# Neighbourhood attention by row groups: taking the groups in twos per head pair, with shared bias tables and keys

## The chip, the core and the metric

One core of one Trainium2 chip runs the whole kernel in one launch, on float32 inputs. The metric is the device time in microseconds (us) of one execution; the time given is the median of the runs. Engines: PE (matrix multiply; PEld is its weight load), DVE (vector), ACT (scalar), POOL (GpSimd), SP (issues nearly all DMAs).

## The reference

One layer (DEPTH is 1): RMSNorm, one projection to q, k, v and gate, 2-D neighbourhood attention on a grid of 32 rows by 64 columns (16 heads of 64), SiLU gate, output projection, residual, final RMSNorm. Shapes: x is (1, 2048, 1024), the projection is 1024 by 4096. Each query sees 8 key rows and 16 key columns around it, with a learned bias per head and offset.

```
def row_fn(r):
    rs = jnp.clip(r - kh // 2, 0, rows - kh)          # kh = 8 key rows
    qr = ...[query row r];  kr, vr = ...[key rows rs .. rs+7, columns around the block]
    s = jnp.einsum('bnqhd,bknjhd->bhnqkj', qr, kr).astype(jnp.float32) * scale
    row_off = rs + jnp.arange(kh) - r + NA_ROWS - 1
    bias = jnp.take(col_bias, row_off, axis=1).transpose(0, 2, 3, 1, 4)
    s = jnp.where(col_valid[None, None], s + bias[None], NEG_INF)
    p = jax.nn.softmax(s.reshape(B, H, nb, NA_QBLOCK, kh * NA_KBLOCK), axis=-1)
    o = jnp.einsum('bhnqkj,bknjhd->bnqhd', p, vr)
x = x + (o * jax.nn.silu(gate)) @ w_out               # then the final rmsnorm
```

## The kernel before

Two stages of projections come first (`stage_one`, `stage_two`, 0 to 562 us of the profiled execution): dense 512-column matmuls in a seven-product scheme, whose results q, k, v and gate go to DRAM (`qd`, `kd`, `vd`, `sgd`). At the end the output projection runs in the same scheme (`rows_by_seven`, from about 878 us). Between them lies the attention stage, 32 **runs**; between the attention's own matmuls a fixed number of dense matmuls is put, first the rest of the projections (`projections`: q, k and gate of head pairs 6 and 7 for the lower half of the grid, 288 matmuls), then the first four output tiles (`outputs`, 192 matmuls).

A run is one head pair `p` (0 to 7) and one **row group** `T` (0 to 3: the 8 query rows 8T to 8T+7 with all 64 columns, 512 queries). A run has two halves of 4 query rows, two quads of 8-column strips, two heads `s`. Its steps:

- `load_k`, `load_q`, `load_v`, `load_sg`, `load_bias` bring keys, queries, values, gate and bias tables by SP. Keys of a run are the key rows `KEY_ROWS[T]`: 11, 15, 15 or 12 rows, each row 64 columns, so (rows x 64 + 8) x 4 bytes x 128 partitions. `kp` has two buffers for them. Bias tables are of three kinds (`TABLES`: "mid" with 11 key rows by 23 columns, "top" and "end" with 8 by 23), one table per quad; group 0 needs top and mid, groups 1 and 2 mid alone, group 3 mid and end. Group 2 takes the tables that group 1 of the same head pair has loaded; the others load all of theirs.
- `scores(i)` for each quad: 16 small matmuls per call and head pair into two banks, then per half and head one `tensor_tensor_reduce` on DVE (line 1314): bank plus bias table goes to the tile `X`, with the row minimum into `st`. The bank is read in its own order (key row outer, column inner, contiguous) and `X` is written column outer, key row inner, so with a step of 11, 12 or 15 elements. Then ACT takes the exponential (line 1320) in place.
- `normalise` multiplies by the reciprocal of the sums (POOL, DVE and ACT, lines 1332 to 1336), `turns` transposes `X` on PE (line 1354, into banks `ph`) and copies to `pta` (DVE and ACT, lines 1358 and 1360), `values` multiplies by `vt` (line 1377), DVE multiplies by the gate into `og` (line 1381), and `keep` stores `og` to `ogd` (SP, line 1384).
- `clear_x` sets to zero (POOL) the parts of `X` that a group's halves don't write. It is called at the start, and where the group's kind changes (two times).

The loop over `m` emits, in this order: `begin(m)` (puts the loads of the next run on a list by due time, counted in dense matmuls), dense matmuls, the rest of `normalise` of run m-1, dense matmuls, `turns(m-1)`, `scores(2m)`, `scores(2m+1)` with `normalise(2m)` in it, `values(m-1)`. So an engine's order is the order written out, and SP issues its DMAs strictly in the order in which their due times came: per run the store of `ogd` (it waits for DVE's `og`), `vt`, tables `em`, `q`, `kt`, `sgt`, and between them what else is due.

The order of runs is

```
order = [(p, 0) for p in range(NP)] + [(p, T) for p in range(NP) for T in (1, 2)] + [(p, 3) for p in range(NP)]
```

and the number of dense matmuls per run is `amount[m]`, 13.5, with 1.5 more or less in turn in runs 8 to 23 (`amount[m] += 1.5 if m % 2 == 0 else -1.5`). The first output tiles need row group 0 of all head pairs: `load_og(0)` and `load_og(1)` (512 KB each, line 1411) are called in the last half of `projections`, `split_og(0)` is put on the list 24 matmuls later with a lag of 9. In the last runs `land_first` and `land_rest` load parts of the output weights into buffers that the attention no longer uses.

Of the kernel before, what the change touches and what calls it, by code (L numbers as in the profile page):

```python
# [22 lines left out]
NK = D // 128  # L23
# [11 lines left out]
KEY_ROWS = [(0, 11), (4, 19), (12, 27), (20, 32)]  # L35
HALF_ROWS = [[(0, 8), (0, 11)], [(0, 11), (4, 11)], [(0, 11), (4, 11)], [(0, 11), (4, 8)]]
# [7 lines left out]
def bias_tables(rpb):  # L44
    out = []
    for q0, k0, n in TABLES.values():
        for quad in range(2):
            got = []
            for g in range(4 * quad, 4 * quad + 4):
                qr, col, kr, c = np.ogrid[q0:q0 + 4, :8, k0:k0 + n, :WIDE]  # L50
# [11 lines left out]
def build(ctx, tc, x, xr, xt, wg, bias, w_out, n0, nf, out):  # L62
# [21 lines left out]
    kp = pool("kp", 2)  # L84
# [4 lines left out]
    def vh(shape, dt, nm):  # L89
        if not vhalf:  # L90
            t = vp([128, 1024], dt, nm)
            vhalf.extend((t[:, :512], t[:, 512:]))
        return vhalf.pop(0)

# [508 lines left out]
    def stage_one():  # L603
# [6 lines left out]
        land["x12"] = [rbp([128, 512], F32, "land") for _ in range(2)] + [kp([128, 1024], F32, "land")[:, :512] for _ in range(2)]  # L610
# [30 lines left out]
        def value_rows(j):  # L641
            spot = mkp([128, 3, 512], F32, "vs")
            homes = [spot[:, k] for k in range(3)] + [kp([128, 1024], F32, "vs")[:, :512]]
# [49 lines left out]
        def step(i):  # L693
# [3 lines left out]
            if i >= 2 * E:  # L697
                seven.after(n, P, then)
            elif P == 1:
                seven.keep(n, kp([128, 1024], F32, "p1")[:, :512] if n > 3 else accs[n - 2] if n > 1 else None)  # L700
# [205 lines left out]
        def load_u1():  # L906
            for t in range(4):
                U1[t] = accs[t] if t < 2 else ep([128, 512], F32, "u1") if t == 2 else kp([128, 1024], F32, "u1")[:, :512]
                nc.sync.dma_start(U1[t], vu1[t])
# [87 lines left out]
    def stage_two():  # L997
# [11 lines left out]
        def out_rows(k):  # L1009
            def g():  # L1010
# [3 lines left out]
                else:  # L1014
                    homes = [rbp([128, 512], F32, "ow") for _ in range(2)]
                homes += [kp([128, 1024], F32, "ow")[:, :512] for _ in range(4 - len(homes))]
# [31 lines left out]
        def also(n, i):  # L1048
            if (n, i) in sums_at:
                sums_at[n, i]()  # L1050
            if n == 0:
                if i == 0:
                    load_ahead()
                elif i == 1:
                    for f in load_bias(0, 0):
                        f()
# [4 lines left out]
                if i == 3:  # L1061
                    load_k(0, 0)()
                    load_q(0, 0)()
# [14 lines left out]
        def values_product(P, i):  # L1078
            if P in (1, 6, 5):
# [5 lines left out]
            if P == 1:  # L1085
                U1[i] = ep([128, 512], F32, "u1") if i < 2 else kp([128, 1024], F32, "u1")[:, :512]
# [117 lines left out]
    order = [(p, 0) for p in range(NP)] + [(p, T) for p in range(NP) for T in (1, 2)] + [(p, 3) for p in range(NP)]  # L1204
    pairs = [(p, T, quad) for p, T in order for quad in range(2)]
    lastp = {T: p for p, T in order}

    def slot(T, p):
        return 7 if p == lastp[T] else p - (p > lastp[T])

    def load_k(p, T):
        r0, r1 = KEY_ROWS[T]
        n = (r1 - r0) * GW
        must(*[("k", p, c) for c in range(r0 // 8, (r1 + 7) // 8)])

        def keys():
            KT[p, T] = t = kp([128, 1024], F32, "kt")
            more = 8 * (r1 < ROWS)
            if not more:
                nc.gpsimd.memset(t[:, n:n + 8], 0.0)  # L1220
            nc.sync.dma_start(t[:, :n + more], kd[p][:, r0 * GW:r1 * GW + more])
# [12 lines left out]
    def load_v(p, T):  # L1234
        r0, r1 = KEY_ROWS[T]
# [3 lines left out]
        nc.sync.dma_start(t[:8 * (r1 - r0)], rows)  # L1239
# [6 lines left out]
    kinds_of = lambda T: {0: ("top", "mid"), 3: ("mid", "end")}.get(T, ("mid", "mid"))  # L1246

    def load_bias(p, T):
        fs = []
        for kind in dict.fromkeys(kinds_of(T)):  # L1250
            w = 2 * WIDE * TABLES[kind][2]
            for quad in range(2):
                t = mp([128, 512], F32, "em")[:, :w]
                for half in range(2):
                    if kinds_of(T)[half] == kind:
                        EM[p, T, quad, half] = [t[:, :w // 2], t[:, w // 2:]]
                o = TABLE_AT[kind] + quad * w
                fs.append(lambda t=t, o=o, w=w: nc.sync.dma_start(t, bias[p, :, o:o + w]))
        if T == 1:
            for quad in range(2):  # L1260
                for half in range(2):
                    EM[p, 2, quad, half] = EM[p, 1, quad, half]
# [4 lines left out]
    def height(T):  # L1267
        return KEY_ROWS[T][1] - KEY_ROWS[T][0]

    def by_column(t, half, T):  # L1270
        u, n = HALF_ROWS[T][half]
        return t[:, :WIDE * height(T)].rearrange("p (c r) -> p c r", r=height(T))[:, :, u:u + n]

    def make_x():
        for half in range(2):
            for quad in range(2):
                for s in range(2):
                    X[quad, half, s] = xp([128, 512], F32, f"x{s}")
        clear_x(0)

    def clear_x(T):
        R = height(T)
        for quad in range(2):
            for half, (u, n) in enumerate(HALF_ROWS[T]):
                a, b = (0, u) if u else (n, R)
                for s in range(2):
                    t = X[quad, half, s]
                    nc.gpsimd.memset(t[:, WIDE * R:(WIDE + 1) * R], 0.0)
                    if a < b:
                        nc.gpsimd.memset(t[:, :WIDE * R].rearrange("p (c r) -> p c r", r=R)[:, :, a:b], 0.0)  # L1290

    def scores(i, between=None):
        p, T, quad = pairs[i]
        kt, qt = KT[p, T], QT[p, T]
        both = [bank(512, f"s{s}") for s in range(2)]
        places = {}
        for half, (u, n) in enumerate(HALF_ROWS[T]):
            for s in range(2):
                places[half, s] = both[s][:, 256 * half:256 * half + WIDE * n]
            for h in range(4):  # L1300
                g = 4 * quad + h
                for s in range(2):
                    a = slice(s * 64, s * 64 + 64)
                    o = u * GW + 8 * FIRST[g]
# [4 lines left out]
        for half, (u, n) in enumerate(HALF_ROWS[T]):  # L1309
            xs_ = [by_column(X[quad, half, s], half, T) for s in range(2)]  # L1310
# [587 lines left out]
```

## Time and profile before

| | |
|---|---|
| time before, median of 3 runs | 997.99 us (995.85 to 999.03) |
| the profiled execution: time, span | 1001.41 us, 999.5 us |
| PE busy | 980.3 us (98%) |
| DVE busy | 782.0 us (78%) |
| ACT busy | 531.7 us (53%) |
| POOL busy | 126.7 us (13%) |
| moved by DMA | 233.94 MB, mean 234 GB/s |
| attention stage | about 562 to 878 us |

Matmuls are pipelined and their ends are modelled, so a PE that is called busy can still lose a little beside a wait. A window's row gives its length, then each engine's busy time with its instructions in brackets, the granted TensorE clock, the mean busy share of the 16 DMA engines and what they moved. A row of a group gives what it writes and reads, partitions by elements, the count, the busy time and the mean time of one in ns, and the engine's idle time before them.

### The profile page before, as it was taken

To read this page: it belongs to the slowest core of one execution; us is meant where nothing else is said; L and a number is where in the kernel's file an instruction comes from. 1 tells how busy PE (TensorE), PEld (TensorE's weight loads), DVE (VectorE), ACT (ScalarE), POOL (GpSimd) and SP (SyncE) were. 2 spreads that over 40 slices of the span, in tenths; PEclk is the share of its full clock that TensorE was granted. 3 is DMA by queue.
4 is the path that set the end of the run, shared out by engine and by line. 5 is a ranking of instruction groups with operands and counts; after the bars stand their busy time and mean duration, and the time that the engine had idled before them with its cause. 6 is when DMAs were issued, how large, how long until landed. Compare 5 with 4: busy or idle time off the path is not lost.

```text
span 999.5 us, 22147 instructions
## 1 busy us (share of the span) xinstructions
PE 980.3 (98%) x8172; PEld 797.8 (80%) x8172; DVE 782.0 (78%) x1703; ACT 531.7 (53%) x1310; POOL 126.7 (13%) x256
## 2 busy tenths in 40 slices
PE   9999999999999999999999999999899999999997
PEld 6888888888888888888888777877677777888886
DVE  5899888987666876766775688888789989986866
ACT  7863245455534433333434476777677776653443
POOL 0000001321100000000000122322122321202110
PEclk9999999999999999999999999999999999999999
DMA  8943547777957845655565899988979999997754
GB/s 291 337 132 91 194 146 248 242 249 262 360 144 225 261 136 181 220 180 189 193 206 176 258 327 302 293 237 258 299 223 287 265 285 287 350 364 202 201 148 116
DMA packets 151084, 233.94 MB, mean 234 GB/s; under 512 B 13568, under 2 KB 66048, under 8 KB 150976
## 3 DMA queue, kind: packets, MB, share of 16 engines
q1 hardware_dynamic: 147952, 227.41, 71.7%
q0 software_dynamic: 2592, 4.72, 2.8%
q8 instruction: 64, 1.05, 0.4%
q10 hardware_dynamic: 432, 0.40, 0.1%
q14 instruction: 44, 0.36, 0.1%
HBM read 166.42 MB, written 66.06 MB: 233 GB/s over the span
## 4 chain that ended last, share of the span: by engine, by line
PE 87%; DMA 9%; ACT 2%; SPq 1%; issue 1%; DVE 0%; POOL 0%; ACTq 0%; POOLq 0%; DVEq 0%
PE pp L432 40%; PE pv L598 13%; PE py L1675 11%; PE o L1377 5%; PE s L1305 4%; DMA kt<-kd 3%; PE ph L1354 3%; PE pv L713 2%; PE pp L378 2%; PE pp L376 2%; PE pp L380 2%; ACT x L1320 1%; DMA t<-wodT 1%; DMA xr<-in_x_dram 1%; DMA sgt<-sgd 1%
## 5 line engine op out<-in xcount | busy, mean ns | idle before, releaser
L432 PE MATMUL pp<-h,f 128*128 128x512 f32 x576 | 185.3, 389 | 0.0
L432 PE MATMUL pp<-t,f 128*128 128x512 f32 x702 | 171.4, 389 | 0.0
L432 PEld LDWEIGHTS pp<-t,f 128*128 128x128 f32 x702 | 131.8, 188 | 27.4
L1320 ACT ACTIVATE x<-x,st 128x253 f32<-128x253 f32 (+1 forms) x256 | 124.4, 491 | 45.7 <-DVE st L1314 45.6
L1314 DVE CUSTOM_DVE_ANT_0 x<-s,em 128x253 f32<-128x253 f32 (+1 forms) x256 | 119.0, 576 | 11.8 <-issue 9.9
L432 PEld LDWEIGHTS pp<-h,f 128*128 128x128 f32 x576 | 108.1, 188 | 22.5
L432 PE MATMUL pp<-l,f 128*128 128x512 f32 x288 | 112.1, 389 | 0.0
L1336 POOL TENSOR_SCALAR x<-x,st 128x253 f32<-128x253 f32 (+1 forms) x160 | 75.8, 492 | 224.4 <-DVE st L1325 209.0
L415 DVE TENSOR_TENSOR f<-raw,f 128x512 fp32r<-128x512 f32 x105 | 75.7, 726 | 19.3 <-ACT f L414 19.2
L1377 PEld LDWEIGHTS o<-pta,vt 120*64 120x64 f32 (+2 forms) x1152 | 70.2, 137 | 20.4 <-issue 12.2
L1377 PE MATMUL o<-pta,vt 120*64 120x192 f32 (+8 forms) x1152 | 84.3, 299 | 1.7 <-issue 1.0
L414 ACT ACTIVATE f<-raw 128x512 fp32r<-128x512 f32 x105 | 63.6, 622 | 37.0 <-DVE raw L421 22.0
L1305 PE MATMUL s<-kt,q 64*32 64x253 f32 (+1 forms) x2048 | 61.3, 369 | 9.3 <-DMA kt<-kd 5.7
L1358 DVE COPY pta<-ph 120x512 f32<-120x512 f32 (+2 forms) x96 | 60.2, 681 | 10.8 <-PE ph L1354 10.4
L1360 ACT ACTIVATE pta<-ph 120x512 f32<-120x512 f32 (+2 forms) x96 | 50.2, 594 | 31.1 <-PE ph L1354 31.0
L432 PEld LDWEIGHTS pp<-l,f 128*128 128x128 f32 x288 | 54.0, 188 | 11.4
L1675 PE MATMUL py<-woh,f 128*128 128x512 f32 x192 | 60.9, 390 | 0.0
L598 PE MATMUL pv<-wh,t 128*128 128x512 f32 x176 | 56.2, 389 | 0.0
L1354 PEld LDWEIGHTS ph<-ident,x 64*120 64x120 f32 (+2 forms) x1536 | 46.2, 128 | 11.7 <-issue 8.5
L1305 PEld LDWEIGHTS s<-kt,q 64*32 64x32 f32 x2048 | 39.2, 107 | 19.7 <-issue 4.7
L432 PE MATMUL pp<-sixths,f 128*128 128x512 f32 x198 | 52.7, 389 | 0.0
L1354 PE MATMUL ph<-ident,x 64*120 64x64 f32 (+2 forms) x1536 | 50.9, 219 | 0.3 <-POOL x L1336 0.3
(230 smaller groups left out, 1871.3 us busy)
## 6 DMA issues: line engine op xcount, KB each, us to landing
raw<-in_wg_dram SPq DMA_DIRECT2D x124, 256.0 KB
em<-in_bias_dram SPq DMA_DIRECT2D x48, 253.0 KB
row<-in_xr_dram SPq DMA_DIRECT2D x32, 256.0 KB
vd<-v SPq DMA_DIRECT2D x32, 256.0 KB
sgd<-sg SPq DMA_DIRECT2D x32, 256.0 KB
q<-qd SPq DMA_DIRECT2D x32, 256.0 KB
sgt<-sgd SPq DMA_DIRECT2D x32, 256.0 KB
ogd<-og SPq DMA_DIRECT2D x32, 256.0 KB
```

The costliest lines, as they stand in the source:

```text
L414: nc.scalar.activation(t[:, 0], src, AF.Copy)
L415: nc.vector.tensor_tensor(t[:, 1], src, t[:, 0].bitcast(F32), OP.subtract)
L432: nc.tensor.matmul(B[n, P], t[:, int(m == 2), c], x[k][int(m == 1)], start=P in (1, 6, 5) and k == 0 and m == 0, stop=k == 3 and m == 2, s ...
L598: nc.tensor.matmul(p, a[:, o], b, start=P in (1, 6, 5) and k == 0 and m == 0, stop=k == 3 and m == 2, skip_group_check=True)
L1305: nc.tensor.matmul(places[half, s][h * 32:h * 32 + 32], qt[a, g * 64 + half * 32:g * 64 + half * 32 + 32], kt[a, o:o + n * GW].rearrange(" ...
L1314: nc.vector.tensor_tensor_reduce(xs_[s].rearrange("p c r -> p r c"), flat(places[half, s]), flat(EM[p, T, quad, half][s]), -1.0, 1e38, OP. ...
L1320: nc.scalar.activation(xs_[s], xs_[s], AF.Exp, bias=st[:, o:o + 1], scale=-1.0, accum_out=st[:, 4 + o:5 + o])
L1336: nc.gpsimd.tensor_scalar(t, t, st[:, o:o + 1], 1.0, op0=OP.mult, op1=OP.mult)
L1354: nc.tensor.transpose(ph[h][:k, o:o + 64], X[quad, half, s][q, at:at + k], ident[q, q])
L1358: nc.vector.tensor_copy(o, i_)
L1377: nc.tensor.matmul(o[s * 64:s * 64 + 64, g0 * 64:g1 * 64], vt[:k, strip, s * 64:s * 64 + 64], moving, start=strip == 0, stop=strip == 7, s ...
L1675: nc.tensor.matmul(B[m, P], t[:, a, c], b, start=P in (1, 6, 5) and k == 0 and i == 0, stop=k == 3 and i == 2, skip_group_check=True)
```

## The change

- The order of runs: per head pair first group 1, then group 0, for all eight; then group 2 and group 3 in the same way, with the last two head pairs as (6,2), (7,2), (7,3), (6,3).
- Bias tables: each run loads one kind only (`BRINGS`), two tables: group 1 and 2 mid, group 0 top, group 3 end; groups 0 and 3 take mid from the run before.
- Keys: groups 1 and 0 of a head pair share one key tile, rows 0 to 18; group 1 loads rows 4 to 18, group 0 adds rows 0 to 3. Groups 2 and 3 share rows 12 to 31 (16 rows, then 4). The tile lies in `kp` (now one buffer of 2048 columns) for even head pairs and in `mkp` for odd ones. Elsewhere the two halves of that one buffer (`kh`) stand in for the two buffers of before.
- One frame: every run takes 15 key rows for `X`, the transposes and the values (`FRAME`, `TALL`), in place of 11, 15, 15 and 12. The halves' key rows stay 8 or 11.
- `tensor_tensor_reduce` writes `X` in its own order (key row inner, runs of 8 or 11 elements side by side) and reads the bank with a step of 23 elements; the tables are stored column outer, key row inner, so they are read in order.
- `clear_x` is called in each run, for the rows alone that the last group wrote and the next doesn't.
- `ogd` is in the order of head pairs (`slot` goes). `amount` is even, and the last entry 6 less. `load_og(0)`, `load_og(1)` get a lag of 20, `split_og(0)` one of 19 in place of 9. `land_first` loads 9 parts in place of 10, `land_rest` 8 in place of 7.

```diff
-KEY_ROWS = [(0, 11), (4, 19), (12, 27), (20, 32)]
-HALF_ROWS = [[(0, 8), (0, 11)], [(0, 11), (4, 11)], [(0, 11), (4, 11)], [(0, 11), (4, 8)]]
+FRAME, TALL = [0, 4, 12, 17], 15
+HALF_ROWS = [[(0, 8), (0, 11)], [(0, 11), (4, 11)], [(0, 11), (4, 11)], [(3, 11), (7, 8)]]
...
-    kp = pool("kp", 2)
+    kp = pool("kp", 1)
...
+    def kh(shape, dt, nm):
+        if not khalf:
+            t = kp([128, 2048], dt, nm)
+            khalf.extend((t[:, :512], t[:, 1024:1536]))
+        return khalf.pop(0)
...
-                        load_og(0)
-                        load_og(1)
+                        store(("ogl",), 20, lambda: (load_og(0), load_og(1)))
                     else:
-                        store(("og0",), 9, lambda: split_og(0))
+                        store(("og0",), 19, lambda: split_og(0))
...
-    order = [(p, 0) for p in range(NP)] + [(p, T) for p in range(NP) for T in (1, 2)] + [(p, 3) for p in range(NP)]
+    order = [(p, T) for p in range(NP) for T in (1, 0)] + [(p, T) for p in range(NP - 2) for T in (2, 3)]
+    order += [(NP - 2, 2), (NP - 1, 2), (NP - 1, 3), (NP - 2, 3)]
...
+    PARTS = {1: (4, 19, 8), 0: (0, 4, 0), 2: (12, 28, 0), 3: (28, 32, 0)}
...
         def keys():
-            KT[p, T] = t = kp([128, 1024], F32, "kt")
-            more = 8 * (r1 < ROWS)
-            if not more:
-                nc.gpsimd.memset(t[:, n:n + 8], 0.0)
-            nc.sync.dma_start(t[:, :n + more], kd[p][:, r0 * GW:r1 * GW + more])
+            if T in (1, 2):
+                khalf.clear()
+                KT[p, T // 2] = (kp([128, 2048], F32, "kt") if p % 2 == 0 else mkp([128, 1536], F32, "kt"))[:, :1344]
+            t = KT[p, T // 2]
+            if T == 2:
+                nc.gpsimd.memset(t[:, 1280:1288], 0.0)
+            nc.sync.dma_start(t[:, a - base * GW:b - base * GW], kd[p][:, a:b])
...
+    BRINGS = {0: "top", 1: "mid", 2: "mid", 3: "end"}
...
     def clear_x(T):
-        R = height(T)
+        stale = []
+        for half in range(2):
+            (u0, n0), (u1, n1) = held[half], HALF_ROWS[T][half]
+            held[half] = u1, n1
+            stale += [(half, a, b - a) for a, b in ((u0, min(u0 + n0, u1)), (max(u0, u1 + n1), u0 + n0)) if a < b]
         for quad in range(2):
-            ...
+            for half, a, n in stale:
                 for s in range(2):
-                    ...
+                    nc.gpsimd.memset(by_column(X[quad, half, s], (a, n)), 0.0)
...
-                nc.vector.tensor_tensor_reduce(xs_[s].rearrange("p c r -> p r c"), flat(places[half, s]), flat(EM[p, T, quad, half][s]), -1.0, 1e38,
+                nc.vector.tensor_tensor_reduce(xs_[s], places[half, s].rearrange("p (r c) -> p c r", c=WIDE),
+                                               table[s].rearrange("p (c r) -> p c r", c=WIDE), -1.0, 1e38,
                                                OP.add, OP.min, st[:, o:o + 1])
...
-        k = 8 * (KEY_ROWS[T][1] - KEY_ROWS[T][0])
+        k = 8 * TALL
...
-        if m + 1 < cycles and order[m + 1][0] == 0 and order[m + 1][1] in (1, 3):
+        if m + 1 < cycles:
             clear_x(order[m + 1][1])
...
-    for m in range(8, 24):
-        amount[m] += 1.5 if m % 2 == 0 else -1.5
...
-            if (*nx, 0, 0) not in EM:
-                later_loads(load_bias(*nx), 3, 1.5)
+            later_loads(load_bias(*nx), 3, 1.5)
```

More of the change, by code (lines that the diff above doesn't have):

```diff
@@ L1054, in also @@
                 elif i == 1:
[L1055 removed]
+                    for f in load_bias(*order[0]):
                         f()
@@ L1572, in outputs @@
             p = bank(512, "po")
-            who = {slot(n // 4, q): q for q in range(NP)}
             for i in range(NK):
                 gh, gl = G[n][i]
-                q = who[i]
-                while (q, j) not in woh:
+                while (i, j) not in woh:
                     consume(1, True)
@@ L1633, in load_rows_of @@
         T, i = divmod(n, 4)
-        must(*[("og", p, T) for p in range(NP) if slot(T, p) // 4 == half])
+        must(*[("og", p, T) for p in range(NP) if p // 4 == half])
         A[m, f] = (home or raw)([128, 512], F32, "raw")
```

105 lines of the change are left out of this document (48 added, 57 removed).

## The prediction

> **What bounds the kernel now.** I read the page's first part, then the busy times by stretch, then the chain of waits, then the groups of the attention stage.
>
> ```profile
> span 999.5 us, 22147 instructions
> ## 1 busy us (share of the span) xinstructions
> PE 980.3 (98%) x8172; PEld 797.8 (80%) x8172; DVE 782.0 (78%) x1703; ACT 531.7 (53%) x1310; POOL 126.7 (13%) x256
> ```
>
> PE works nearly all the time, and the change takes no matmul away. So only PE's idle time can be won, 19.2 us in all. The stretches show where it lies: before attention, the four blocks of eight attention runs, and the end.
>
> ```profile
> 0.00:562.00 562.00, 560.57 (x2467) 461.55 (x2475) 422.58 (x679) 255.31 (x484) 32.00 (x37) 1.00 0.66 213
> 561.90:641.40 79.50, 77.57 (x1290) 61.38 (x1289) 64.79 (x206) 56.64 (x178) 18.86 (x44) 1.00 0.95 303
> 641.40:719.90 78.50, 74.80 (x1296) 58.87 (x1293) 66.57 (x204) 57.75 (x176) 20.82 (x55) 1.00 0.92 268
> 719.90:800.10 80.20, 76.53 (x1292) 59.77 (x1293) 69.84 (x210) 58.52 (x179) 20.77 (x58) 0.98 0.88 259
> 800.10:864.70 64.60, 63.33 (x1137) 51.27 (x1138) 58.38 (x202) 44.28 (x150) 16.05 (x41) 1.00 0.95 297
> 864.70:999.50 134.80, 127.56 (x710) 105.09 (x708) 99.80 (x204) 59.31 (x146) 18.16 (x23) 0.99 0.73 218
> ```
>
> Length minus PE's busy time gives 1.4 us ahead of attention, then 1.93, 3.70, 3.67 and 1.27 (10.6 us in the attention blocks), and 7.2 at the end, mostly the tail behind the last matmul. In attention the DMA engines are busy 88 to 95% of the time; elsewhere 66 to 73%. What PE waits for:
>
> ```profile
> PE s L1305 <- DMA kt<-kd: 5.7, 5, 2.8
> PE s L1305 <- issue: 3.5, 2, 2.7
> PE o L1377 <- issue: 1.0, 1, 1.0
> PE o L1377 <- ACT pta L1360: 0.8, 1, 0.8
> PE ph L1354 <- POOL x L1336: 0.3, 1, 0.3
> ```
>
> So the loss is keys that land late. Single attention runs, from one group of scores to the next, show how it is spread (the first two are group 0; then groups 1, 2, 2, 2, 1, 2):
>
> ```profile
> 584.68:594.78 10.10, 8.92 (x165) 7.14 (x162) 8.88 (x28) 7.71 (x24) 2.26 (x5) 1.00 1.03 342
> 594.78:605.18 10.40, 9.65 (x162) 7.45 (x162) 6.58 (x24) 5.72 (x20) 2.25 (x5) 1.00 0.89 278
> 659.96:668.88 8.92, 8.92 (x165) 7.04 (x161) 7.38 (x25) 7.25 (x23) 2.44 (x5) 1.00 0.77 218
> 668.88:678.48 9.60, 9.60 (x168) 7.60 (x164) 8.67 (x27) 7.22 (x23) 2.44 (x5) 1.00 0.91 254
> 687.39:698.62 11.23, 10.22 (x167) 7.79 (x164) 9.20 (x28) 7.87 (x24) 2.45 (x5) 1.00 0.89 251
> 708.22:719.92 11.70, 8.99 (x164) 7.06 (x161) 9.16 (x27) 7.48 (x23) 2.46 (x5) 1.00 1.02 324
> 719.92:730.48 10.56, 10.56 (x160) 7.97 (x160) 7.04 (x24) 6.08 (x20) 2.45 (x5) 0.84 0.84 232
> 787.67:800.13 12.46, 9.69 (x167) 7.38 (x163) 11.38 (x31) 8.34 (x25) 3.66 (x23) 1.00 0.97 263
> ```
>
> A clean run has no PE idle at all: 8.92 us for group 1, 9.60 for group 2 with three matmuls more, so 0.23 us per dense matmul. A disturbed one loses 0.8 to 2.8 us of idle and a little more, since a matmul drawn across a stall counts as busy (10.22 us at 687 with one matmul less than the clean 9.60: 0.6 hidden). After the long stall at 717 the granted clock was 0.84 and that run took 10.56 in place of 8.92: 1.6 us more.
>
> **The change, part by part.**
>
> **Bytes.** Sizes follow from the code (columns x 512 bytes), and three rows anchor them:
>
> ```profile
> em<-in_bias_dram SPq DMA_DIRECT2D x48, 253.0 KB
> ...
> kt<-kd SPq DMA_DIRECT2D x16, 484.0 KB
> vt<-vd SPq DMA_DIRECT2D x16, 480.0 KB
> ```
>
> Tables before, per head pair: three pairs of mid (6 x 253), one of top and one of end (4 x 184), 2254 KB; after, two pairs of mid and one each of top and end, 1748. Keys: 356 + 484 + 484 + 384 = 1708 KB; after, 484 + 128 + 512 + 128 = 1252. Values: 352 + 480 + 480 + 384 = 1696; after, 4 x 480 = 1920. Net 738 KB less per head pair, 5.9 MB of some 85 MB that the four attention blocks move (their GB/s times their lengths): 7%. Fewer DMAs too: 64 tables in place of 80.
>
> Per run, with queries, gate and the store of the output (768 KB): before 2350, 2238, 1732, 2410 KB for groups 0 to 3; after 1744, 2238, 2266, 1744. So the heavy blocks, where each run asks for 2.4 MB, go, and everything looks like the middle blocks of today, where 2.24 and 1.73 alternate. That lightens the first and the last block, and the change of block at 787 to 800, where keys waited behind four tables. It doesn't lighten the middle. I take as gone the idle of the two group-0 runs (1.18 + 0.75), of the run at 787 (2.77) and of the last block (1.27), 6.0 us, and 1.2 hidden beside it (0.3 for each of four stalls, half of the 0.6 above): -7.2. Bounds: nothing, if each is replaced by a stall of the middle kind, and all 10.6 + 1.6 + hidden 2 = -14.2.
>
> **What stays.** The worst stall of the middle, with SP's issues ahead of it (start, length):
>
> ```profile
> 708.19 0.90 SPq L1411 DMA_DIRECT2D ograw<-ogd  x2
> 709.13 0.65 SPq L1221 DMA_DIRECT2D kt<-kd  x1
> ```
>
> Keys queue behind 1 MB for the output tiles, and scores come 2.7 us late (the 708 row), with the slow clock behind it: 4.3 us. The new lag of 20 moves these two loads to a run or two later, since group 0 now ends with run 15. There they stand right behind the store of run 15's `ogd`, which they must see landed; SP stands still for that time, and queued behind it are that run's `q` and `kt`. So I keep 4.3 us (bounds 1 and 7), and the 1.0 at 687 and smaller ones. What is late next is the keys of groups 1 and 2, still the last large DMA of each burst. Against the change: their burst now falls into a run of 13.5 dense matmuls with a group 0 or 3, about 9 us, before into one of 9.60.
>
> **Splits.** `split_og(0)` is now emitted 5 matmuls ahead of its use (before 15), which is 1.1 us, and its copies stand in ACT's and DVE's queue ahead of a `normalise`. Before, one split cost PE 0.3 us (last row of the waits above). I take +0.7, bounds 0 and 2.
>
> **Transposes** get 15 rows everywhere:
>
> ```profile
> L1354 PE MATMUL ph<-ident,x 64*120 64x64 f32 x768 | 26.2, 221 | 0.3 <-POOL x L1336 0.3
> ...
> L1354 PE MATMUL ph<-ident,x 64*96 64x64 f32 x384 | 12.4, 218 | 0.0
> L1354 PE MATMUL ph<-ident,x 64*88 64x64 f32 x384 | 12.3, 218 | 0.0
> ```
>
> 384 transposes of 120 columns hold PE 13.1 us, of 96 12.4, of 88 12.3. Nothing hides PE's own work: +1.5 us. Scores keep their halves of 8 and 11 rows. Values contract over 120 rows in place of 88 or 96 with the same moving columns: nothing.
>
> **Strided bank reads.** Today's read of the bank is in order and the write to `X` steps 44 to 60 bytes; after, the read steps 92 bytes and the write is in order.
>
> ```profile
> L1314 DVE CUSTOM_DVE_ANT_0 x<-s,em 128x253 f32<-128x253 f32 x192 | 97.1, 606 | 9.6 <-issue 8.3 <-PE s L1305 1.0
> ...
> L445 DVE TENSOR_TENSOR u<-pp,p 128x512 f32<-128x512 f32 x38 | 26.1, 687 | 13.2 <-PE pp L432 13.1
> ...
> L421 DVE TENSOR_TENSOR s<-raw 128x512 f32<-128x512 f32 x21 | 14.4, 685 | 4.9 <-DMA raw<-in_wg_dram 4.9
> ```
>
> Line 445 reads a bank with a step of 8 elements (32 bytes) and takes 687 ns for 512, as line 421 does from contiguous SBUF: a strided bank read is free there. Line 1314 takes 606 ns for 253, far more per element, so its strided write may be what costs. Per run it holds DVE 3.91 us, and ACT's exponentials behind it 4.12:
>
> ```profile
> 668.88:678.48 9.60, 3.91 (x16) 1.00 0.91 254
> 668.88:678.48 9.60, 4.12 (x16) 1.00 0.91 254
> ```
>
> (the first row is line 1314, the second line 1320). Were it faster, ACT would set the pace of the chain, and PE, which waits for it in no clean run, would win nothing; DVE's `og`, for which SP's store waits, would come up to a microsecond earlier, which only helps the keys. I take 0; lower bound -2 (keys earlier), upper bound +18 (the rival below).
>
> [...]
>
> **POOL.** `clear_x` grows from three calls to one per run, with 8 memsets where group 0 or 3 follows and 4 or none elsewhere.
>
> ```profile
> L1290 POOL MEMSET x<- 128x92 f32 x12 | 2.0, 186 | 2.8 <-PE ph L1354 2.8
> ```
>
> At most 8 x 0.186 = 1.5 us; about 0.6 by the run at 787, where 16 of them made POOL's time 3.66 in place of 2.44. They follow the last transpose, and each reduction on DVE needs its own tile's alone, so DVE would wait for the first, 0.2 us; queued behind them on POOL is `normalise`, which waits for DVE anyway. Cost nothing; if the cover were gone, 0.2 us a run, 6 in all.
>
> **Values' DMA** grows by 224 KB per head pair, which the bytes above hold. [...]
>
> **Edits with one answer, 0 us.** Key buffers still alternate, `kp` for even and `mkp` for odd head pairs. `kh` makes some loads of the first stages wait for two readers in place of one; there PE idles 1.4 us in 562 and the loads are asked for several products ahead. The `slot` order, the even `amount`, the 6 matmuls moved behind the last run and `land_first` shift no PE work.
>
> **Sum.** -7.2 + 1.5 + 0.7 + 0 = -5.0 us. The profiled execution took 1001.41 us, 3.4 above the median of 997.99; I set the sum against its stalls and take the difference off the median: 993.0.
>
> **The rivals.** (1) *The relief is eaten.* The keys of groups 1 and 2 stall in the outer blocks about half as often as in the middle now (half of 3.7 us of idle for each 8 runs, twice), while the rest goes as above: -5.0 + 3.7 = -1.3, 996.7. For it: the middle stalls with the least bytes per run. Against it: runs from 641 to 687 go clean with the same load. (2) *Late keys everywhere:* every block idles like the middle ones, 4 x 3.7 = 14.8 against 10.6 now, with 1.5 for transposes and a second stall with the slow clock (1.6): +7.3, 1005. It decides once a heavy burst (2.27 MB with about 0.6 MB of other loads) needs more than the 9 us run, which is 320 GB/s; the block of group 0 shows 303 on average and 342 at its best. (3) *The strided read slows line 1314*, the other side by one mechanism: with 0.15 us more for each of 8, the chain to the transposes grows by 1.2 us. The clean runs give no idle at all, so what slack they have lies below that; with 0.6 us of it, half of the 1.2, the price is 0.6 x 31 = 18 us, 1016. It decides from 0.6 / 8 = 0.07 us each. Against it: line 445.
>
> **How the numbers follow.** Forecast (985 to 995) 0.56, rival 1 0.22, rival 2 0.14, rival 3 0.08. Within 0.3% is 3 us, about what a measurement of this kernel can tell from no change. Faster 0.56, same 0.22, slower 0.22. The low end takes all stalls gone, -14.2 + 1.5 = 985; the high end takes in rivals 1 and 2 and leaves out rival 3 and the worst of the rest: 985 to 1005. The forecast's own range is 985 to 995.
>
> **What would show it.** Right: the stretches of the first and last eight runs with under 1 us of PE idle each, no key wait at a change of block, transposes at 52.4 us in all, tables with 64 issues, DMA share in attention under 0.9. Line 1314 under 606 ns shows the write to have been the cost, above it the read. Wrong: new waits of `s` for `kt` in every second run, PE waiting for `X` at line 1354, or a stall over 4 us behind the moved `ograw` loads.

## The result, and the profile after

| | before | after |
|---|---|---|
| median of 8 runs | 999.15 us (995.85 to 1003.75) | 993.10 us (991.71 to 994.65) |
| the profiled execution: time, span | 1001.41, 999.5 us | 991.77, 989.8 us |
| ratio after / before (95%) | | 0.9931 (0.9908 to 0.9954) |

The changed kernel is faster by 0.7%. The first part of its page:

```profile
span 989.8 us, 22264 instructions
## 1 busy us (share of the span) xinstructions
PE 979.6 (99%) x8172; PEld 797.4 (81%) x8172; DVE 757.3 (77%) x1703; ACT 532.5 (54%) x1310; POOL 148.1 (15%) x396
```

PE does the same 8172 matmuls in 0.7 us less; idle time went from 19.2 to 10.2 us. Together these are the 9.7 us between the two spans. The same stretches as before show where (length, busy time by engine, clock, DMA share, GB/s):

```profile
0.00:562.50 562.50, 561.03 (x2459) 461.44 (x2459) 424.47 (x679) 255.48 (x484) 32.77 (x33) 1.00 0.67 212
562.50:642.00 79.50, 79.17 (x1296) 62.30 (x1297) 59.59 (x206) 57.64 (x178) 25.77 (x86) 1.00 0.92 271
642.00:714.70 72.70, 72.70 (x1299) 57.94 (x1300) 57.01 (x203) 55.51 (x175) 25.49 (x91) 1.00 0.90 273
714.70:789.70 75.00, 74.18 (x1296) 58.82 (x1294) 61.31 (x210) 57.77 (x180) 24.84 (x94) 1.00 0.94 289
789.70:855.80 66.10, 64.69 (x1136) 51.70 (x1132) 55.73 (x205) 46.71 (x152) 21.04 (x74) 1.00 0.86 258
855.80:989.80 134.00, 127.83 (x712) 105.16 (x708) 99.21 (x204) 59.36 (x146) 18.23 (x23) 0.99 0.72 214
```

The four attention stretches idle 0.33, 0, 0.82 and 1.41 us, 2.6 in all; before it was 1.93, 3.70, 3.67 and 1.27, 10.6 in all. The clock is 1.00 in all four. So the gain was where the prediction looked for it, in attention, but not only in the blocks it named: the second and third stretches, which it left as they were but for one stall, are nearly free of idle time too.

What PE still waits for in attention:

```profile
PE s L1311 <- DMA kt<-kd: 1.7, 2, 1.4
PE s L1311 <- PE ph L1361: 0.5, 1, 0.5
PE po L1588 <- DVE gl L1431: 0.2, 1, 0.2
```

Late keys, 5.7 us before and the stall of 2.7 that stood under "issue", are down to 1.7, or 2.2 with the wait of 0.5 put down to `ph` (PE's own work), which was for keys too, as the part on the prediction shows. The longest stall left, 1.4 us, ends at 809.2, and SP's issues (start, length) and its wait show where it comes from:

```profile
789.47 0.32 SPq L1255 DMA_DIRECT2D sgt<-sgd  x1
796.32 0.33 SPq L1422 DMA_DIRECT2D xr<-in_x_dram  x1
...
797.23 0.57 SPq L1391 DMA_DIRECT2D ogd<-og  x1
797.89 0.68 SPq L1250 DMA_DIRECT2D vt<-vd  x1
798.62 0.47 SPq L1269 DMA_DIRECT2D em<-in_bias_dram  x1
799.14 0.49 SPq L1241 DMA_DIRECT2D q<-qd  x1
799.73 0.38 SPq L1232 DMA_DIRECT2D kt<-kd  x1
```

```profile
SPq L1422 <- ACT xr L1463: 6.7, 2, 6.2
```

SP issues nothing from 789.8 to 796.3: its next DMA overwrites `xr`, and for 6.2 us it waits for ACT to be done with it. After that the run's store, its `vt`, a table and `q` go ahead of the keys. The keys are last in the order in which SP gives out a run's loads, apart from the gate, so whatever holds SP up holds up the keys.

One group changed in itself, the reduction on DVE:

```profile
L1320 DVE CUSTOM_DVE_ANT_0 x<-s,em 128x253 f32<-128x253 f32 x192 | 70.0, 415 | 5.9 <-issue 4.0 <-PE s L1311 1.3
```

It took 606 ns with the bank read in order and the stepped write to `X`; with the stepped read of the bank and the write in order it takes 415.

### The profile page after: what moved, and what is told of

It reads as the page before. It is cut to its first block, busy times and chain, and to the rows that moved or that the text cites. A ratio compares the mean times of both kernels' runs of the same rounds, so it can differ in the third digit from the quotient of the medians.

```text
span 989.8 us, 22264 instructions
## 1 busy us (share of the span) xinstructions
PE 979.6 (99%) x8172; PEld 797.4 (81%) x8172; DVE 757.3 (77%) x1703; ACT 532.5 (54%) x1310; POOL 148.1 (15%) x396
## 2 busy tenths in 40 slices
DMA packets 149228, 227.89 MB, mean 230 GB/s; under 512 B 13312, under 2 KB 65792, under 8 KB 149120
## 4 chain that ended last, share of the span: by engine, by line
PE 95%; DMA 3%; ACT 1%; DVE 1%; issue 0%; SPq 0%; ACTq 0%
PE pp L440 40%; PE pv L606 13%; PE py L1681 12%; PE o L1384 7%; PE s L1311 5%; PE ph L1361 4%; PE pv L721 2%; PE pp L384 2%; PE pp L388 2%; PE pp L386 2%; DMA kt<-kd 2%; PE po L1586 1%; PE po L1590 1%; PE po L1588 1%; DMA xr<-in_x_dram 1%; ACT x L1327 1%
## 5 line engine op out<-in xcount | busy, mean ns | idle before, releaser
L1343 POOL TENSOR_SCALAR x<-x,st 128x253 f32<-128x253 f32 (+1 forms) x160 | 78.5, 510 | 130.5 <-DVE st L1332 127.1
L1320 DVE CUSTOM_DVE_ANT_0 x<-s,em 128x253 f32<-128x253 f32 (+1 forms) x256 | 87.3, 398 | 6.6 <-issue 4.5
L1384 PEld LDWEIGHTS o<-pta,vt 120*64 120x64 f32 x1152 | 70.0, 137 | 18.4 <-issue 12.0
L1384 PE MATMUL o<-pta,vt 120*64 120x192 f32 (+2 forms) x1152 | 84.1, 299 | 0.0
L1365 DVE COPY pta<-ph 120x512 f32<-120x512 f32 x96 | 60.3, 684 | 13.6 <-PE ph L1361 13.1
L1367 ACT ACTIVATE pta<-ph 120x512 f32<-120x512 f32 x96 | 50.5, 599 | 33.8 <-PE ph L1361 33.6
L1311 PE MATMUL s<-kt,q 64*32 64x253 f32 (+1 forms) x2048 | 58.7, 362 | 2.2 <-DMA kt<-kd 1.7
L1361 PEld LDWEIGHTS ph<-ident,x 64*120 64x120 f32 x1536 | 47.6, 135 | 11.3 <-issue 10.6
L461 POOL TENSOR_TENSOR tmp<-tmp,rb 128x512 f32<-128x512 f32 x18 | 28.4, 1580 | 158.0 <-DVE tmp L458 138.3
L1361 PE MATMUL ph<-ident,x 64*120 64x64 f32 x1536 | 52.0, 221 | 0.0
```

Of the source, the lines that this page charges most:

```text
L1311: nc.tensor.matmul(places[half, s][h * 32:h * 32 + 32], qt[a, g * 64 + half * 32:g * 64 + half * 32 + 32], kt[a, o:o + n * GW].rearrange(" ...
L1320: nc.vector.tensor_tensor_reduce(xs_[s], places[half, s].rearrange("p (r c) -> p c r", c=WIDE), table[s].rearrange("p (c r) -> p c r", c=W ...
L1343: nc.gpsimd.tensor_scalar(t, t, st[:, o:o + 1], 1.0, op0=OP.mult, op1=OP.mult)
L1361: nc.tensor.transpose(ph[h][:k, o:o + 64], X[quad, half, s][q, at:at + k], ident[q, q])
L1365: nc.vector.tensor_copy(o, i_)
L1384: nc.tensor.matmul(o[s * 64:s * 64 + 64, g0 * 64:g1 * 64], vt[:k, strip, s * 64:s * 64 + 64], moving, start=strip == 0, stop=strip == 7, s ...
```

## The experiments

What had to be told apart: is the gain due to the bytes (tables and keys shared), to the faster reduction, to the new places of the dense matmuls and of `ograw`, or is all of this only a way of getting the keys earlier, which could be had directly by the order of SP's loads? The ratios, each against runs of the kernel before on the same chip (95%), follow. Three chips were used (e1 to e4; e5 to e8 and e12; e9 to e11), so between them the ratios compare better than the medians.

| run | starts from | ratio | median us |
|---|---|---|---|
| the change | | 0.9931 (0.9908 to 0.9954) | 993.1 |
| e1, reduction as before | after | 0.9962 (0.9942 to 0.9981) | 995.5 |
| e2, fast reduction alone | before | 0.9997 (0.9972 to 1.0023) | 999.0 |
| e3, fewer table bytes alone | before | 0.9971 (0.9947 to 0.9996) | 995.4 |
| e4, bytes put back | after | 1.0086 (1.0064 to 1.0108) | 1008.0 |
| e5, fast reduction and fewer bytes | before | 0.9919 (0.9891 to 0.9946) | 992.5 |
| e6, places alone | before | 0.9959 (0.9930 to 0.9988) | 996.2 |
| e7, as many bytes again away | after | 0.9899 (0.9858 to 0.9940) | 991.5 |
| e8, keys first | after | 0.9874 (0.9837 to 0.9911) | 988.5 |
| e9, keys first | before | 0.9913 (0.9883 to 0.9943) | 991.1 |
| e10, keys first, reduction as before | after | 0.9920 (0.9893 to 0.9947) | 991.7 |
| e11, keys first, bytes put back | after | 1.0057 (1.0032 to 1.0081) | 1005.6 |
| e12, keys first, fast reduction | before | 0.9918 (0.9893 to 0.9942) | 989.3 |

**e1: the change without the faster reduction.** Tables are laid out and the bank is read as before, `X` is written with the step.

```
-  nc.vector.tensor_tensor_reduce(xs_[s], places[half, s].rearrange("p (r c) -> p c r", c=WIDE),
-                                 table[s].rearrange("p (c r) -> p c r", c=WIDE), -1.0, 1e38,
+  nc.vector.tensor_tensor_reduce(xs_[s].rearrange("p c r -> p r c"), places[half, s].rearrange("p (r c) -> p r c", c=WIDE),
+                                 table[s].rearrange("p (r c) -> p r c", c=WIDE), -1.0, 1e38,
```

> The changed kernel with one part undone: the reduction again reads the bank in order and writes X with a step (now 15 elements, 60 bytes); tables stored to match; all else as changed. Theory R (the gain is fewer bytes and no heavy bursts, so keys land in time): the reduction goes back to about 600 ns for 253, but the time stays within 2 us of the changed kernel (about 993 to 995). Theory S (the gain is the faster reduction, which lets the output store and so SP's later loads go earlier): 4 to 6 us are given back (997 to 999). Theory O (the gain is the order of runs, the even amounts and the later loads for the output tiles): as the changed kernel, within 1 us.

Its reduction, and PE's largest wait in attention (total, times, longest):

```profile
L1320 DVE CUSTOM_DVE_ANT_0 x<-s,em 128x253 f32<-128x253 f32 x192 | 96.7, 602 | 5.6 <-issue 4.4 <-PE s L1311 0.6
```

```profile
PE s L1311 <- DMA kt<-kd: 2.7, 3, 1.1
```

The reduction is back at 602 ns, so of the two steps the write's is the costly one, and everything else is that of the changed kernel. By the ratios some 0.31% (3 us) of the gain is lost, between theory R's 2 us and theory S's 4 to 6; the two intervals overlap, and the profiled execution lost only 1.1 us of span. So the fast reduction may be a part of the gain, but this run does not show it for certain.

**e2: the faster reduction alone.** The same edit the other way round, in the kernel before.

> The kernel before with the strided bank read alone (tables stored column outer to match): order, bytes and frames as before. Theory R: the reduction falls to about 415 ns for 253, the time by 0 to 2 us, and the late keys (about 10 us of PE idle in attention) stay. Theory S: 4 to 6 us faster than before. Theory O: no change.

The reduction and PE's largest waits in attention:

```profile
L1313 DVE CUSTOM_DVE_ANT_0 x<-s,em 128x253 f32<-128x253 f32 x192 | 70.2, 416 | 7.0 <-issue 5.1 <-PE s L1305 1.7
```

```profile
PE s L1305 <- DMA kt<-kd: 5.6, 4, 1.9
PE o L1377 <- issue: 2.8, 1, 2.8
```

DVE is relieved as in the changed kernel, and the time doesn't move: 0.9997 (at most 0.3% by the interval). The keys are as late as before (5.6 us). Here DVE's speed is worth nothing by itself.

**e3: fewer bytes alone.** Only the "mid" tables are loaded, and groups 0 and 3 use them in place of their own, so the right bias of these groups is left out: 5.9 MB of tables less, as much as the change saves in all.

```
-  for kind in dict.fromkeys(kinds_of(T)):
-      w = 2 * WIDE * TABLES[kind][2]
...
+  w = 2 * WIDE * TABLES["mid"][2]
...
+      v = WIDE * TABLES[kinds_of(T)[half]][2]
+      EM[p, T, quad, half] = [t[:, :v], t[:, v:2 * v]]
```

> The kernel before with fewer bytes alone: groups 0 and 3 load the mid tables only and read the shapes of top and end from the same tiles, so 368 KB less in each of 16 runs, 5.9 MB in all, the same sum as the change saves; the bias of these groups is left out of the right values. Order, amounts and read of the bank as before. Theory R: 4 to 7 us faster than before, idle of the first and last block nearly gone, the middle blocks' idle (7.4 us) unchanged. Theory S: 0 to 2 us. Theory O: 0 to 2 us.

PE's largest waits in attention:

```profile
PE s L1304 <- DMA kt<-kd: 2.2, 2, 1.2
PE s L1304 <- DVE pta L1357: 1.4, 2, 1.1
```

Late keys shrink from 5.7 to 2.2 us, and 1.4 us of waits for DVE's copies take up part of it. 0.29% (2.9 us; 0.4 to 5.3 by the interval) of the 0.69% is had by bytes alone, less than the 4 to 7 us that theory R expected.

**e4: the changed kernel with the bytes put back.** The "top" and "end" tables are loaded twice.

```
+  for again in range(1 if kind == "mid" else 2):
```

> The changed kernel with the bytes put back: groups 0 and 3 load their two tables twice, 368 KB more in each of 16 runs, 5.9 MB in all, spread evenly over every second run; the second copy is the one that is read. Theory R: 4 to 7 us slower than the changed kernel (997 to 1000), with new waits for keys. Theory S and theory O: within 2 us of the changed kernel.

PE's only kind of wait in attention:

```profile
PE s L1313 <- DMA kt<-kd: 12.1, 7, 4.2
```

15 us slower than the change (median 1008.0 against 993.1), where theory R had 4 to 7, and slower than the kernel before, which moves the same number of bytes (233.9 MB both). About a third of the 15 us is not idle time: over the attention stage PE idles 9.6 us more than in the changed kernel and is busy 5.6 us longer with about the same matmuls, at a granted clock of 0.98, 1.00, 0.96 and 0.98 in the four stretches. So the pairing of row groups by itself is no gain: without the saved bytes the paired order is slower than the old one.

**e5: both, in the kernel before.** e2 and e3 together, with the tables of e3.

> The kernel before with two parts of the change: strided bank read and 5.9 MB less of tables (groups 0 and 3 read the shapes of top and end from mid tiles, so their bias is left out of the right values). Order of runs, frames, amounts, places of the loads as before. Theory R2 (bytes and the faster reduction together are the gain; the reduction helps only once the DMA queue has room): 5 to 7 us faster than before, like the whole change. Theory O2 (half or more of the gain is the new order with its even bursts): 2 to 4 us faster, as with the bytes alone, with stalls of over 1 us left in runs 13 to 23.

PE's two largest waits in attention:

```profile
PE s L1304 <- issue: 2.4, 1, 2.4
PE s L1304 <- DMA kt<-kd: 1.2, 3, 0.5
```

0.9919 is as much as the whole change: the old order, the old frames and the old places, with two edits alone. Beside e2 (nothing) and e3 (0.29%, on another chip) the two together give 0.81%, more than their sum, if the intervals are taken at their middle. What is left is a stall of 2.4 us that ends at 716, behind the `ograw` loads.

**e6: the places alone.** The kernel before with even amounts, the two lags of the change and 6 matmuls moved behind the last run.

```
-  load_og(0)
-  load_og(1)
+  store(("ogl",), 20, lambda: (load_og(0), load_og(1)))
-  store(("og0",), 9, lambda: split_og(0))
+  store(("og0",), 19, lambda: split_og(0))
-  for m in range(8, 24):
-      amount[m] += 1.5 if m % 2 == 0 else -1.5
```

> The kernel before with the schedule edits alone: even amounts of dense matmuls, the first loads for the output tiles 20 later, the first split at 19, 6 matmuls less in the last entry. Order, bytes and read as before. Theory O3 (these places are a part of the gain, since 1 MB of loads no longer stands ahead of keys at 708): 2 to 4 us faster, the stall of runs 15 and 16 gone. Theories R2 and O2: within 2 us of before; the stall moves with the loads by one or two runs.

PE's two largest waits in attention:

```profile
PE s L1304 <- DMA kt<-kd: 3.8, 4, 1.4
PE o L1376 <- issue: 2.4, 2, 1.5
```

0.41% faster, with every byte and the slow reduction kept: the longest single wait for keys is 1.4 us in place of 2.8, and none is followed by a slow clock (1.00 over the whole stage in the profiled execution). e5 and e6 together hold all the parts that were tried alone, and their gains would add up to 1.22%, where the whole change has 0.69%. So either the parts overlap and relieve the same late keys, or the new order costs something of its own; these runs don't tell the two apart.

**e7: still fewer bytes.** The changed kernel with no "top" and "end" tables at all, groups 0 and 3 use parts of the "mid" ones.

```
+  if kind != "mid":
+      w = WIDE * TABLES[kind][2]
+      EM[p, T // 2, kind] = [[t[0][:, :w], t[1][:, :w]] for t in EM[p, T // 2, "mid"]]
+      return fs
```

> The changed kernel with yet 5.9 MB less: groups 0 and 3 load no tables and read the shapes of top and end from the mid tiles, so their bias is left out of the right values. With the run that had 5.9 MB put back (15 us slower than the changed kernel) this gives a scale. Theory K (the gain bends: past some load the keys are late, below it nothing is left to win): 2 to 4 us faster than the changed kernel, the rest of its key waits gone, 989 to 991. Theory L (time goes with bytes): again 10 us or more, 983 or less.

991.5 against 993.1: another 5.9 MB bring 1.6 us, less than theory K's 2 to 4 and within the noise (the intervals overlap), where the same 5.9 MB in the other direction (e4) cost 15. The changed kernel stands just behind the bend: in this order of loads the bytes have done about what they can.

**e8: keys first.** In the changed kernel only due times are changed: queries and keys of a run go ahead of the tables and ahead of the store on SP, and the first split of `ograw` is due 5 matmuls earlier.

```
-  later_loads([load_q(*nx), load_k(*nx)], 7, 5)
-  later_loads(load_bias(*nx), 3, 1.5)
+  later_loads([load_q(*nx), load_k(*nx)], 2, 1)
+  later_loads(load_bias(*nx), 7, 3)
-  store(("og0",), 19, lambda: split_og(0))
+  store(("og0",), 14, lambda: split_og(0))
```

> The changed kernel with queries and keys of the next run due 2 and 3 matmuls into a run, ahead of the store that SP waits for, tables at 7 and 10, and the first split for the output tiles 5 matmuls earlier. If what is left (about 4 us of stalls in attention) is keys behind other loads: 2 to 3 us faster than the changed kernel, 990 to 991, no wait for keys left. If the queue as a whole is too full: no change, and the waits go to tables or queries.

SP's issues of one run (start, length), and the four stretches of attention:

```profile
644.48 0.33 SPq L1241 DMA_DIRECT2D q<-qd  x1
644.85 0.43 SPq L1232 DMA_DIRECT2D kt<-kd  x1
647.77 0.56 SPq L1391 DMA_DIRECT2D ogd<-og  x1
```

```profile
562.50:642.00 79.50, 79.50 (x1286) 62.54 (x1286) 60.20 (x207) 57.16 (x177) 25.64 (x85) 1.00 0.92 272
642.00:714.60 72.60, 72.60 (x1294) 57.83 (x1290) 56.86 (x203) 55.44 (x175) 25.50 (x89) 1.00 0.93 273
714.60:789.00 74.40, 74.40 (x1330) 59.45 (x1334) 62.31 (x212) 58.61 (x182) 25.38 (x96) 1.00 0.95 287
789.00:853.00 64.00, 64.00 (x1130) 51.06 (x1116) 54.93 (x204) 46.09 (x151) 20.72 (x70) 1.00 0.91 269
```

The keys now leave 2.9 us ahead of the store that SP must wait for. PE has no idle time left in attention (length and busy time agree in all four rows), though the DMA engines are at least as busy as in the changed kernel. With 0.9874 (988.5 us) this is the best version, 4.6 us under the change by the medians.

**e9: keys first in the kernel before.** The same two lines there (tables at 7 and 1.5).

> The kernel before with the due times alone: queries and keys of the next run due 2 and 3 matmuls into a run, tables from 7 on; order, bytes, read as before. Theory P (PE lost its time to keys that stood behind other loads and behind the store that SP waits for; bytes only set how far back they stood): 6 to 9 us faster than before, no wait for keys left. Theory R2 (the queue as a whole was too full for the old order): 0 to 3 us faster, with waits for tables, values or gate in place of those for keys.

The first stretch of attention, and PE's largest waits in the stage:

```profile
561.90:641.00 79.10, 78.02 (x1305) 61.52 (x1310) 65.31 (x206) 56.93 (x179) 19.24 (x49) 1.00 0.99 311
```

```profile
PE o L1377 <- issue: 1.5, 2, 1.1
PE o L1377 <- ACT pta L1360: 0.8, 1, 0.8
```

0.9913 with all the bytes, the slow reduction and the old order: no wait for keys is left, while the DMA engines are 99% busy in the first eight runs. Two lines of due times do as much as the whole change. In the old order a full DMA queue wasn't the loss; the place of the keys in it was. The traces' semaphore records, which tell when each load landed, show how far the keys moved (medians over 31 of the 32 attention runs, the first left out). Before, keys were issued 9.6 us ahead of their scores, took 7.8 us to land and landed 1.4 us ahead; here they are issued 14.2 us ahead, take 6.6 and land 7.2 ahead. In the changed kernel they land only 1.5 us ahead, in e3 2.0, in e8 7.9. The edit moves the keys both ahead of other loads and earlier in time; these two are not told apart.

**e10: keys first, reduction as before.** e8 with the edit of e1.

> The changed kernel with keys first and the first split earlier (988.5 us), and the reduction reading the bank in order again (about 600 ns for 253). Theory P: as with the strided read, within 1.5 us, since PE no longer waits for keys, whenever the store goes. Theory S2 (the slower reduction costs time by itself): 2 to 4 us slower.

0.9920 against 0.9874 for e8, with intervals that overlap (on two chips), and with profiled executions of the same span, 987.1 us. By the medians that is 3.2 us (theory S2's range), by the ratios 4.6; whether any of it is the reduction's stays open.

**e11: keys first, bytes put back.** e8's order of loads with e4's double tables, which follow each other at 1.5 matmuls in place of 3.

> The changed kernel with keys first and the 5.9 MB of tables put back (with keys late these bytes cost 15 us). Theory P: within 3 us of keys first without them (988 to 992). Theory R2: 8 us slower or more, with waits moved to tables or values.

PE's largest waits in attention, and DVE's wait for tables:

```profile
PE o L1386 <- DMA vt<-vd: 4.6, 4, 2.1
PE o L1386 <- issue: 2.9, 2, 1.6
```

```profile
DVE x L1322 <- DMA em<-in_bias_dram: 18.1, 15, 2.8
```

By theory P the keys' order would have taken this kernel near e8; theory R2 came true. The order took back 2.4 of e4's 15 us: the keys are no longer late, but now `vt` and the tables are. In the pairs' order a queue with 5.9 MB more is too full as a whole, and the order only chooses who waits. The kernel before carries those bytes with keys first (e9). Between the two stand 96 tables of which 64 are small in place of 80 with 32 small, even `vt` loads of 480 KB and another spread over the runs; which of these is the cause wasn't tried.

**e12: keys first and the fast reduction in the kernel before.** e9 and e2 together.

> The kernel before with keys first and the strided bank read, in the old order, with the old bytes, frames and places: is the new order needed? If the new order adds something beside room for the keys: slower than the changed kernel with keys first (988.5), about 990 to 992, with idle left in the heavy first block. If not: 987 to 989, since it saves 1.3 us of longer transposes.

The whole attention stage as one stretch:

```profile
562.00:865.00 303.00, 301.83 (x5205) 239.21 (x5203) 243.83 (x850) 224.75 (x709) 79.58 (x201) 1.00 0.96 297
```

1.2 us of idle time in 303, and 0.9918 (989.3 us): no different from e9 or e10. Its median is 0.8 us above e8's on the same chip, between the two ranges that were expected; the ratios are 0.44% apart, with intervals that overlap. With the keys first the shared tables and keys are worth nothing that these runs resolve.

## Why the prediction was right, step by step

The time came out at 993.1 where 993.0 was forecast. The reason given is half right. Late keys were the loss: moving them alone (e8, e9) takes the waits away. Fewer bytes do help, but alone they brought 2.9 us (e3), where their term was -7.2; the reduction (e5 beside e3, at the middle of the intervals) and the places (e6), which stood in the sum with 0, had a part in the rest.

That the number agrees so well is partly luck. The sum was -5.0; the medians moved by 6.05 (999.15 to 993.10), and the median of three runs from which the forecast started (997.99) is 1.2 under that of eight. In the profiled pair the change brought 9.6 us (1001.41 to 991.77), but that pair says too much: the execution before lies 2.3 above its median, the one after 1.3 below.

- **Bytes.** The 5.9 MB worked out were 5904 KB of 1024 bytes; the page's 233.94 - 227.89 = 6.05 MB are the same in MB of a million bytes. The DMA engines' share times length over the four blocks fell from 280 to 266 us, 4.9%; the bytes moved there (GB/s times length) from 85.1 to 80.1 MB, 5.8%. What the larger `vt` loads cost beyond their bytes no run isolates. By the semaphore records of both executions every one of the 32 `vt` loads has 9 updates, the first 1.1 to 1.7 us after the start of its issue, and every one of the 32 key loads 16, the first 2.2 us after it or later.
- **The heavy blocks, -7.2.** Of the 1.93 of the first block 1.6 went, and the 2.77 of the change at 787 went as well. The 1.27 of the last block did not: 1.41 is there now, behind SP's pause shown above, so "under 1 us in the last eight runs" missed. It lies within a block of groups 2 and 3; at the change of block (scores at 714.66) no key wait is left, as said.
- **What stays** is the term that was mis-sized. The prediction kept the middle's stalls and 4.3 us for the `ograw` loads. The mechanism was as described; SP's queue after:

```profile
720.00 0.57 SPq L1391 DMA_DIRECT2D ogd<-og  x1
720.66 0.68 SPq L1250 DMA_DIRECT2D vt<-vd  x1
721.39 0.48 SPq L1269 DMA_DIRECT2D em<-in_bias_dram  x1
725.03 0.81 SPq L1418 DMA_DIRECT2D ograw<-ogd  x2
725.89 0.42 SPq L1241 DMA_DIRECT2D q<-qd  x1
726.35 0.51 SPq L1232 DMA_DIRECT2D kt<-kd  x1
```

```profile
SPq L1418 <- DMA ogd<-og: 3.1, 1, 3.1
```

  SP stood 3.2 us (721.87 to 725.03) for the store to land, with `q` and `kt` queued behind it. The scores that need this `kt` start at 733.50, after a wait of 0.5 us. The view puts that wait down to `ph`, but by the semaphore records PE's sequencer waits there from 732.23 to 733.44 for just these two loads, and this `kt` lands at 733.40. So the predicted wait came, but with 0.5 us in place of 2.7, and no slow clock behind it (granted clock 1.00): 0.5 in place of 4.3, below the lower bound (1). The sum, which kept the 4.3, leaves out these 3.8 us of gain. The wait is shorter because this `kt` landed 7.1 us after its issue, the one at 709.13 before after 10.7; why it landed sooner the runs tell only in part. With the places alone (e6) the longest wait for keys is 1.4 us in place of 2.8; bytes and reduction together (e5) leave a stall of 2.4 behind these loads at their old place. That points to the new places, but the order of runs differs from e5 as well.
- **Splits, +0.7.** 0.2 us are visible (the wait of line 1588). Within the bounds.
- **Transposes, +1.5.** One group now, of 15 rows throughout:

```profile
L1361 PE MATMUL ph<-ident,x 64*120 64x64 f32 x1536 | 52.0, 221 | 0.0
```

  52.0 us against 26.2 + 12.4 + 12.3 = 50.9: +1.1, and 52.4 had been said.
- **Strided bank reads, 0.** Reading line 445 as the nearest row was right: the stepped write was the price, 606 ns with it and 415 with the write in order and the bank read in steps of 92 bytes. What the stepped read costs by itself isn't shown, since no run has both sides in order. In a clean run DVE's part fell and ACT's stayed (reduction, then exponentials):

```profile
659.80:668.90 9.10, 2.88 (x16) 1.00 0.77 205
659.80:668.90 9.10, 4.12 (x16) 1.00 0.77 205
```

  before 3.91 and 4.12. Alone the edit brings nothing (e2), which fits what was said, that ACT would set the chain's pace. But beside fewer bytes it was worth 3 us by e1 and 5 by e5 less e3, both give or take 3 or more, where the lower bound was 2. `og` is stored earlier, and SP comes free earlier: its waits on the line of the store add up to 81.3 us in the changed kernel and 96.7 in e1. The keys, though, land 1.5 us ahead of their scores (median) in both, so how this turns into time stays open. That it matters only while keys stand behind the store fits e12, where the fast reduction adds nothing to e9.
- **POOL, 0.** 176 memsets, 112 of them in this group, and no wait of PE or DVE names them:

```profile
L1296 POOL MEMSET x<- 128x69 f32 x112 | 12.8, 172 | 45.9 <-PE ph L1361 45.5 <-POOL x L1296 0.2 <-issue 0.2
```

- **DMA share under 0.9** was not met: 0.92, 0.90, 0.94, 0.86. As a sign it was ill chosen, since the stage got shorter with its bytes; e9 has 0.99 and no late key.
- **The rivals.** Rival 1 (the relief is eaten) and 3 (the read is slow) did not come. Rival 2 (late keys everywhere) is real, but lies 5.9 MB away: e4 came to 1008.0, where 1005 had been worked out for the bytes of the changed kernel. The forecast gave it 0.14 at a point that the bend of e4 and e7 shows to be close by.

What the prediction overlooked is the cheapest cure. It named the keys' place behind four tables, behind 1 MB of `ograw` and behind the store, and then counted bytes; by e9 the place alone was worth as much as the whole change.

## What to carry to other kernels

Where one engine issues all loads in order, look at who stands last in each burst and behind which waiting instruction, and move the load that is needed first to the front before saving bytes: two due times were worth 0.87% here (0.9913, 0.9883 to 0.9943), the rebuilt sharing of tables and keys 0.69%, both together 1.26% (0.9874, 0.9837 to 0.9911, so not clearly more than the due times alone). Gains that feed one slack need not add up: the reduction and the bytes were worth 0 and 0.3% alone and 0.8% together, the places 0.4%, and all of them in the new order 0.7%. And the price of bytes bends: 5.9 MB more cost 15 us, 5.9 MB fewer brought 1.6. In e9 the DMA engines were 99% busy in the first eight runs and PE waited for no key, so here a busy share near 1 did not show that transfers were the bound; ask which transfer is late.

## What the runs showed of the hardware

The reduction on DVE from a bank and an SBUF table takes 602 to 606 ns for 253 elements with a write to SBUF that steps 44 to 60 bytes, and 415 to 416 with the write in order and a bank read that steps 92 bytes; the read of its accumulator behind it falls from 153 to 83 ns. The granted clock of 0.84 in the run that starts at 719.92 before is a mean: it was at 0.52 for the first 3.5 us after the wait of 2.7 us, and at 0.99 after that (723.40 to 730.48). So this stall cost more than half of its length again (0.48 x 3.5 = 1.7 us). But the length of the wait didn't decide it here: the wait of 2.8 us that ends at 800.13 in the same execution was followed by the full clock.

```profile
719.92:723.40 3.48, 3.48 (x64) 2.15 (x64) 1.46 (x7) 0.83 (x3) 0.00 (x0) 0.52 1.05 272
800.13:803.60 3.47, 3.47 (x92) 2.95 (x94) 2.33 (x11) 1.68 (x7) 0.00 (x0) 1.00 0.97 268
```

In e4 the clock was 1.00 in the one stretch of attention in which PE has no idle time (642.0 to 715.8), and 0.98, 0.96 and 0.98 in the three in which it idles 3.2, 5.1 and 3.8 us.
